# Which of two large buffers holds the block sums and which the residual rows in the last matrix product of a decoder layer

## The chip, the core and the metric

The kernel runs on one core of one Trainium2 chip. The metric is the device time of the whole kernel in microseconds (us), the median of several runs of the same program. Before the change the three runs gave 1966.43, 1971.43 and 1974.03 us, so the median is 1971.43 us.

A core has engines that run at the same time, each through its own list of instructions in order: TensorE (PE, matmul, with its weight loads shown as PEld), VectorE (DVE), ScalarE (ACT), GpSimd (POOL) and SyncE (SP). In this kernel SP, POOL and ACT also issue transfers (DMA). Engines wait for each other through semaphores.

## What is computed

The reference is one layer of a decoder on 1024 rows of 1024 float32 numbers. Everything but its last step is left as it is by the change. The last step is the end of a gated feed-forward block and a layer norm over the residual sum:

```python
def conv_ffn(h, w_up, dw_w, dw_b, w_down):
    u = causal_dwconv(h @ w_up, dw_w, dw_b)
    gate, val = jnp.split(u, 2, axis=-1)
    return (jax.nn.silu(gate) * val) @ w_down
...
ffn = conv_ffn(h, w_ffn_up[l], ffn_dw_w[l], ffn_dw_b[l], w_ffn_down[l])
h = layer_norm(DN_ALPHA * h + ffn, ln2_g[l], ln2_b[l])
```

`silu(gate) * val` is 1024 rows by 2816 channels, and `w_down` is 2816 by 1024. `h` on the right-hand side is what this page calls the residual rows.

## The kernel before

**The stages.** The kernel normalises the input, runs the mixing part in two halves of 512 rows, projects it back, then does the feed-forward block: the *up phase* (`up_first`, `up_rest`, 22 turns, one for each 128 gate channels with their value channels) and the *down phase* (`down`). Every float32 operand is split into a high part (a cast on ACT) and a low part (a subtraction on DVE), and each product is three matmuls: high times high, high times low, low times high (`mm3`, L170, L171, L172).

**The down phase.** The product with `w_down` is made with seven block products in place of eight. Rows are cut into an early and a late half, channels and output columns into two halves each. Blocks of the activations were written to memory by the up phase (`b11_scr`, `b2_scr`, `t1_scr`, `t32_scr`). The seven products (numbered 0 to 6 here) run one after the other; each has `NK` = 11 steps `k` of 128 channels, and a step is 12 matmuls of 512 columns: four row blocks `t`, three matmuls each. They accumulate in two sets of four banks: `X` (tiles named `acc`) and `Y` (tiles named `sm`, which the up phase uses too).

**One step.** `load(p, k)` (L1024) makes the operands of a step and is traced at a high priority:

- SP loads the activation block and a block of `w_down` into a raw tile `dr` of 512 KB (L1040, L1043). There are five raw tiles: three of the pool `wst` and two of the pool `up`, all shared with the up phase.
- In the products 0, 1, 4 and 5, POOL loads a second block of 256 KB into a tile called `other`, named `do` in the profile (L1049). There are four such tiles: two of the pool `up`, shared with the up phase, and two of the pool `down`.
- In product 0, DVE adds the two weight blocks into `c3[k]`; in product 1 into `c4[k]` (L1012). The sums are weights of later products: `c3` of the products 2 and 3, `c4` (after `c3` has been added) of product 6.
- ACT casts the raw tile into the high half of a weight tile `w_dn` (L1077), and DVE subtracts to get the low half (L1078). There are six weight tiles: three of the pool `wsp`, shared with the up phase, and three of the pool `down`. The steps 0, 1, 2 and every second step after that take one of `wsp`.

A raw tile can be loaded anew only when the cast, the subtraction and the addition that read it are done.

**The large buffers.** The pool `big` has two buffers of 4 MB (32 KB on each of 128 partitions). In the up phase one holds `h1b1`, which only `up_first` reads, and the other `h1b2`, which the fourth product of every turn of `up_rest` reads. `up_first` runs ahead and ends first, so the buffer of `h1b1` is given up first and the buffer of `h1b2` almost at the end of the up phase. In `down` the first large tile that is asked for takes the former, the second one the latter. Before the change these are `rows`, the 1024 residual rows (eight loads of 512 KB by POOL, L1007), and `c3`, the eleven sums of 256 KB. A third large tile, `last`, is asked for in product 6 (L1065); it holds the weights of its last four steps and takes the buffer of `c3` when all that is in it has been read.

**The pool `down`.** It lies on memory that the pool `ffq` of the up phase gives up: the block sums `h1s1` to `h1s3`, read until late in the up phase, and four small tiles `first`, done with when the last `up_first` has been stored. Its tiles are laid out in the order in which they are first asked for: ten sums of `c4`, the statistics, the gain and bias rows (`ln_g`, `ln_b`), `other`, then the weight tiles.

**The residual sum.** After product 0, `one(t)` (L1100, four DVE instructions, L1095) multiplies the early half of rows 0 to 511 by alpha and adds the bank `X[t]`. Functions of the same kind follow the other products; the last of them end in the layer norm and the stores (`ln_out`).

**What sets the order.** All loops are unrolled. A planner simulates the program at build time and puts each engine's instructions into one fixed list, higher priority first among those that could run by its simulation. On the chip each engine then goes through its list in order, so an instruction that waits holds up everything behind it on its engine. A DMA that waits for a buffer holds up the queue that issues it.

Of the kernel before, what the change touches and what calls it, by code (L numbers as in the profile page):

```python
# [8 lines left out]
F32 = mybir.dt.float32  # L9
F32R = mybir.dt.float32r  # L10
# [6 lines left out]
P = 128  # L17
D = 1024
T = 1024
HALF = 512  # L20
# [25 lines left out]
RW_ING, RW_INB, RW_1G, RW_1B, RW_2G, RW_2B = (i * D for i in range(6))  # L46
# [9 lines left out]
def kernel(  # L56
# [16 lines left out]
    V, A, G, TE, SY = nc.vector, nc.scalar, nc.gpsimd, nc.tensor, nc.sync  # L73
# [25 lines left out]
    later = statep.tile([P, P], F32, name="later")  # L99
# [42 lines left out]
    def weights(src, name, keep=None, kept=None):  # L142
        with tc.high_priority(offset=4000):
            st = wst.tile([P, D], F32, tag="st", name=f"st_{name}")
            SY.dma_start(st, src)
            w = wsp.tile([P, 2, D], F32R, tag="w", name=f"w_{name}")
            A.copy(w[:, 0, :], st)  # L147
            if kept is not None:
                SY.dma_start(w[:, 1, :].bitcast(F32), kept)
            else:  # L150
                V.tensor_tensor(  # L151
                    out=w[:, 1, :], in0=st, in1=w[:, 0, :].bitcast(F32), op=ALU.subtract
                )
            if keep is not None:
                SY.dma_start(keep, w[:, 1, :].bitcast(F32))
        return w

    def col_weights(hh, ct):
        scr = low_scr.get(ct)
        return weights(  # L160
            wcol[ct], f"c{hh}_{ct}", None if hh else scr, scr if hh else None
        )

    def big_tile(name):
        return big.tile([P, 2, KD, HALF], F32R, tag="big", name=name)
# [39 lines left out]
    def row(pl, start, n, name, tag=None, eng=SY):  # L205
        r = pl.tile([P, n], F32, tag=tag or name, name=name)
        eng.dma_start(r, prow[start : start + n].partition_broadcast(P))
        return r
# [781 lines left out]
    def down(upp, dp):  # L990
# [6 lines left out]
        def flat_big(name):  # L997
            return big_tile(name).bitcast(F32).rearrange("p i k t -> p (i k t)")

        rows, kept = flat_big("rows"), flat_big("c3")  # L1000
        c3 = [kept[:, k * HALF : (k + 1) * HALF] for k in range(NK)]
        c4 = [dp.tile([P, HALF], F32, name=f"c4_{k}") for k in range(NK - 1)]
        c4.append(upp.tile([P, HALF], F32, tag="s3", name="c4_last"))
        rs = [rows[:, t * D : (t + 1) * D] for t in range(8)]
        sts = [dp.tile([P, 2, 6], F32, name=f"st_f{t}") for t in range(8)]
        for t in range(8):
            G.dma_start(rs[t], h1_scr[t * P : (t + 1) * P, :])  # L1007
        g, b = (row(dp, w, D, n, eng=G) for w, n in ((RW_2G, "ln2_g"), (RW_2B, "ln2_b")))
        E, L = slice(0, HALF), slice(HALF, D)

        def add(dst, x, y):
            V.tensor_tensor(out=dst, in0=x, in1=y, op=ALU.add)  # L1012

        n_steps, n_raw, n_other = 0, 0, 0

        def raw(name):
            nonlocal n_raw
# [1 line left out]
            pl, tag, bufs = ((wst, "st", 3), (upp, "raw", 2))[n_raw % 5 in (1, 3)]  # L1019
            return pl.tile([P, D], F32, tag=tag, bufs=bufs, name=f"{name}_{n_raw}")  # L1020

        last = []

        def load(p, k):  # L1024

            nonlocal n_steps, n_other
            a11, a21, a12, a22 = (wdown[h * NK + k, :, cs] for h in range(2) for cs in (E, L))
            x = (
                b11_scr[k],
                b2_scr[k][:, E],  # L1030
                t32_scr[k][:, L],
                t32_scr[k][:, E],
                t1_scr[k],
                b2_scr[k][:, E],
                b2_scr[k][:, L],
            )[p]
            with tc.high_priority(offset=4000):
                st = raw("dr")
                w_st = st[:, E]
                SY.dma_start(st[:, L], x)  # L1040
                w_of = (a11, a12, a22, None, a21, a22, None)[p]
                if w_of is not None:
                    SY.dma_start(w_st, w_of)  # L1043
                o_of = (a21, a22, None, None, a22, t32_scr[k][:, L], None)[p]
                if o_of is not None:
                    n_other += 1
                    pl, tag = ((dp, "other"), (upp, "s"))[n_other % 2]
                    other = pl.tile([P, HALF], F32, tag=tag, bufs=2, name=f"do{p}_{k}")
                    G.dma_start(other, o_of)  # L1049
                if p < 2:  # L1050
                    add((c3, c4)[p][k], w_st, other)
                elif p == 2:
                    add(w_st, w_st, c3[k])
                elif p == 3:
                    w_st = c3[k]
                    add(c4[k], c4[k], c3[k])
                elif p == 4:
                    add(w_st, w_st, other)
                elif p == 5:
                    add(st[:, L], st[:, L], other)  # L1060
                else:
                    w_st = c4[k]
                if p == 6 and k >= NK - 4:
                    if not last:
                        last.append(big_tile("last").rearrange("p i k t -> p (i k t)"))  # L1065
                    w = last[0][:, (k - NK + 4) * 2 * D : (k - NK + 5) * 2 * D]
                    w = w.rearrange("p (i n) -> p i n", i=2)
                else:
                    own = n_steps % 2 and n_steps > 2
                    w = (dp if own else wsp).tile(  # L1070
                        [P, 2, D], F32R, tag="w", bufs=3, name=f"w_dn{p}_{k}"
                    )
                cuts = ((slice(0, D), st),) if w_st is not c3[k] and w_st is not c4[k] else (
                    (E, w_st), (L, st[:, L])
                )
                for cs, src in cuts:
                    A.copy(w[:, 0, cs], src)  # L1077
                    V.tensor_tensor(  # L1078
                        out=w[:, 1, cs], in0=src, in1=w[:, 0, cs].bitcast(F32), op=ALU.subtract
                    )  # L1080
            n_steps += 1
            return w
# [17 lines left out]
        def one(t):  # L1100
            own(X[t], rs[t], E, ALU.add)
# [34 lines left out]
        for p, (banks, first, then) in enumerate(products):  # L1136
            end = NK - LAST if p == 6 else NK
            for k in range(end):
                w = load(p, k)
                for t in range(4):  # L1140
                    block(banks[t], w, t, first, k)
            ws = {k: load(p, k) for k in range(end, NK)}
            for t in range(4):
                for k in ws:
                    block(banks[t], ws[k], t, first, k)
                then(t)

    def ln_out(dp, t, r, g, b, st):

# [11 lines left out]
    with pool("rows0") as pl:  # L1161
        rs = [pl.tile([P, D], F32, name=f"r0_{t}") for t in range(4)]
# [4 lines left out]
    mixT, _ = combine(1, hT, yT, accs)  # L1167
# [15 lines left out]
    upp = ctx.enter_context(pool("up"))  # L1183
# [5 lines left out]
    dp = ctx.enter_context(pool("down", side="right"))  # L1189
# [100 lines left out]
```

## Time and profile before

| what | value |
|---|---|
| runs | 1966.43, 1971.43, 1974.03 us; median 1971.43 us |
| the profiled execution's own time | 1972.21 us |
| its span (first to last instruction) | 1970.1 us |
| granted TensorE clock, mean | 0.996 |
| end of the up phase's last matmul, from the span's start | about 1751 us |
| last matmul of the kernel | about 1959 us |

The profile is of one execution. Its span lies 2.1 us under that execution's own time. It gives, for each engine, how long it was busy, a view in 40 slices, the chain of work that ended last, and groups of instructions by source line. Further views list single instructions in order of time (a timeline; the note in square brackets is how long the engine stood idle before the instruction, and what released it), sum up waits between engines, or give the busy time of each engine in stretches that the reader names. In names such as `c<-dr,do` the tile that is written stands before the arrow. A matmul is shown as 0.39 us long, but they are pipelined: in undisturbed stretches one starts every 0.227 us.

### The profile page before, as it was taken

To read this page: it belongs to the slowest core of one execution; us is meant where nothing else is said; L and a number is where in the kernel's file an instruction comes from. 1 tells how busy PE (TensorE), PEld (TensorE's weight loads), DVE (VectorE), ACT (ScalarE), POOL (GpSimd) and SP (SyncE) were. 2 spreads that over 40 slices of the span, in tenths; PEclk is the share of its full clock that TensorE was granted. 3 is DMA by queue.
4 is the path that set the end of the run, shared out by engine and by line. 5 is a ranking of instruction groups with operands and counts; after the bars stand their busy time and mean duration, and the time that the engine had idled before them with its cause. 6 is when DMAs were issued, how large, how long until landed. Compare 5 with 4: busy or idle time off the path is not lost.

```text
span 1970.1 us, 25840 instructions
## 1 busy us (share of the span) xinstructions
PE 1932.9 (98%) x9453; PEld 1575.2 (80%) x9453; DVE 1600.7 (81%) x2224; ACT 1083.8 (55%) x1617; POOL 203.1 (10%) x246
## 2 busy tenths in 40 slices
PE   9999999999899999999999999999999999999997
PEld 8888777777688788888778888888888888878886
DVE  7599999999786547898999655587788888879778
ACT  4676767653263265868775435365555555544432
POOL 0001010110310000110101040001000000121010
PEclk9999999999999999999999999999999999999999
DMA  7645455546455665555554644576455555588673
GB/s 270 221 171 198 161 206 177 166 162 202 157 187 176 215 221 182 190 184 198 178 178 148 213 162 129 169 255 227 160 166 183 175 185 184 179 293 297 201 230 125
DMA packets 128416, 378.36 MB, mean 192 GB/s; under 512 B 15104, under 2 KB 15648, under 8 KB 128288
## 3 DMA queue, kind: packets, MB, share of 16 engines
q1 hardware_dynamic: 109152, 321.63, 48.7%
q0 software_dynamic: 12800, 43.54, 6.4%
q10 hardware_dynamic: 6336, 11.54, 1.6%
q8 instruction: 74, 1.21, 0.3%
q14 instruction: 54, 0.44, 0.1%
HBM read 289.99 MB, written 86.65 MB: 191 GB/s over the span
## 4 chain that ended last, share of the span: by engine, by line
PE 71%; DVE 16%; issue 5%; DMA 5%; ACT 2%; POOL 1%; SPq 0%; DVEq 0%; ACTq 0%; POOLq 0%
PE acc L172 16%; PE acc L171 16%; PE acc L170 16%; PE sm L171 6%; PE sm L172 6%; PE sm L170 6%; DVE c L453 5%; DVE w_c L151 1%; DVE x L408 1%; DMA rstd<-nrm_scr 1%; PE sm L536 1%; DMA dr<-wdown 1%; PE sm L539 1%; DVE x L588 1%; DMA b_scr<-fo 1%
## 5 line engine op out<-in xcount | busy, mean ns | idle before, releaser
L170 PE MATMUL acc<-hT,w_c 128*128 128x512 f32 x1000 | 391.8, 392 | 0.5 <-ACT x L406 0.5
L171 PE MATMUL acc<-hT,w_c 128*128 128x512 f32 x1000 | 390.7, 391 | 0.0
L172 PE MATMUL acc<-hT,w_c 128*128 128x512 f32 x1000 | 390.1, 391 | 0.6 <-DVE w_c L151 0.5
L453 DVE SCALAR_TENSOR_TENSOR c<-v,pc,c 128x512 f32<-128x512 f32 x480 | 370.6, 798 | 7.3 <-ACT c L442 4.7
L170 PEld LDWEIGHTS acc<-hT,w_c 128*128 128x128 f32 x1000 | 187.8, 188 | 41.7 <-issue 1.9
L172 PEld LDWEIGHTS acc<-hT,w_c 128*128 128x128 f32 x1000 | 187.8, 188 | 41.2 <-DVE w_c L151 1.4
L171 PEld LDWEIGHTS acc<-hT,w_c 128*128 128x128 f32 x1000 | 187.8, 188 | 39.2 <-issue 1.1
L147 ACT CAST w_c<-st_c 128x1024 fp32r<-128x1024 f32 x128 | 133.8, 1045 | 108.5 <-PE acc L172 90.0
L515 POOL TENSOR_TENSOR ce<-ce,xbc 128x1024 f32<-128x1024 f32 x28 | 74.1, 2648 | 694.3 <-ACT ce L514 694.3
L1077 ACT CAST w_dn<-dr 128x1024 fp32r<-128x1024 f32 (+1 forms) x73 | 68.8, 944 | 87.5 <-DMA dr<-wdown 25.3
L504 ACT ACTIVATE m<-ab,acs 128x128 f32<-128x128 f32 x256 | 78.4, 390 | 48.2 <-PE sm L536 47.0
L170 PE MATMUL sm<-h1s,w_s 128*128 128x512 f32 x264 | 102.7, 389 | 0.0
L171 PE MATMUL sm<-h1s,w_s 128*128 128x512 f32 x264 | 102.7, 389 | 0.0
L172 PE MATMUL sm<-h1s,w_s 128*128 128x512 f32 x264 | 102.2, 389 | 0.0
L151 DVE TENSOR_TENSOR w_c<-st_c,w_c 128x1024 fp32r<-128x1024 f32 x64 | 79.1, 1239 | 22.3 <-ACT w_c L147 22.1
L1078 DVE TENSOR_TENSOR w_dn<-dr,w_dn 128x1024 fp32r<-128x1024 f32 (+1 forms) x73 | 78.7, 1089 | 5.3 <-ACT w_dn L1077 5.3
L408 DVE SCALAR_TENSOR_TENSOR x<-u,pc,x 128x512 f32<-128x512 f32 x96 | 76.7, 810 | 5.7 <-ACT x L406 5.7
L172 PE MATMUL acc<-h1b,w_ue 128*128 128x512 f32 x176 | 68.9, 395 | 1.5 <-DVE w_ue L151 1.5
L170 PE MATMUL acc<-h1b,w_ue 128*128 128x512 f32 x176 | 68.8, 391 | 0.0
L171 PE MATMUL acc<-h1b,w_ue 128*128 128x512 f32 x176 | 68.6, 390 | 0.0
L170 PE MATMUL sm<-h1b,w_s 128*128 128x512 f32 x176 | 68.5, 389 | 0.0
L171 PE MATMUL sm<-h1b,w_s 128*128 128x512 f32 x176 | 68.5, 389 | 0.0
(324 smaller groups left out, 4542.3 us busy)
## 6 DMA issues: line engine op xcount, KB each, us to landing
st_c<-wcol SPq DMA_DIRECT2D x128, 512.0 KB, 4.4
low_scr<-w_c SPq DMA_DIRECT2D x64, 512.0 KB, 2.9
w_c<-low_scr SPq DMA_DIRECT2D x64, 512.0 KB, 4.4
ab<-acs_scr SPq DMA_DIRECT2D x32, 512.0 KB, 4.1
dr<-wdown SPq DMA_DIRECT2D x55, 256.0 KB, 4.8
st_wo<-wo SPq DMA_DIRECT2D x24, 512.0 KB, 4.0
st_ue<-wup SPq DMA_DIRECT2D x22, 512.0 KB, 4.2
first_scr<-first ACTq DMA_DIRECT2D x44, 256.0 KB, 2.9
```

Source lines behind the costliest of these rows:

```text
L147: A.copy(w[:, 0, :], st)
L151: V.tensor_tensor(out=w[:, 1, :], in0=st, in1=w[:, 0, :].bitcast(F32), op=ALU.subtract)
L170: TE.matmul(ps, wa(0), xa(0), start=start, stop=False, skip_group_check=more)
L171: TE.matmul(ps, wa(0), xa(1), start=False, stop=False, skip_group_check=more)
L172: TE.matmul(ps, wa(1), xa(0), start=False, stop=stop, skip_group_check=more)
L408: V.scalar_tensor_tensor(out=o, in0=u[:, k : k + HALF], scalar=pc[:, wc + k : wc + k + 1], in1=o, op0=ALU.mult, op1=ALU.add,)
L453: V.scalar_tensor_tensor(out=accs[i], in0=v[:, k : k + HALF], scalar=pc[:, wc + k : wc + k + 1], in1=accs[i], op0=ALU.mult, op1=ALU.add,)
L504: A.activation(out=m[:, h, :], in_=ab[:, h, :], func=AF.Relu, scale=-1.0, bias=acs[:, c, 8 * g + h : 8 * g + h + 1],)
L515: G.tensor_tensor(out=ce, in0=ce, in1=CT[:, cs].unsqueeze(1).to_broadcast([P, 8, P]), op=ALU.mult)
L536: TE.matmul(o, xs[:, h * HP : (h + 1) * HP], m[:, h, :], start=True, stop=first)
L1077: A.copy(w[:, 0, cs], src)
L1078: V.tensor_tensor(out=w[:, 1, cs], in0=src, in1=w[:, 0, cs].bitcast(F32), op=ALU.subtract)
```

## The change

`c3` now takes the large buffer that is given up first and `rows` the other one. `c3` needs 22 of its 32 KB, so the first two sums of `c4` move into the same buffer, behind the eleven of `c3`. The four `other` tiles are now all of the pool `down`; the two of the pool `up` are no longer used for this. To place them, the first weight tile of `down` (`first_own`) is asked for ahead of them, which puts the `other` tiles at the end of the pool, on the memory of the four `first` tiles. The weight tiles then lie on the memory of `h1s2` and `h1s3`.

The residual rows and the gain and bias rows are no longer loaded at the beginning of `down` but in product 1, after `load(1, 2)`; a dependence without a semaphore (`issue_after`) keeps their ten DMAs behind the `other` load of that step in POOL's list. `one(t)` moves from the end of product 0 to step 7 of product 1.

```diff
+    def issue_after(later, earlier):
+
+        tc.add_manual_dep(
+            later.ins,
+            earlier.ins.name,
+            mybir.DependencyInfo(mybir.DependencyClass.NoSync, mybir.DependencyReason.DATA),
+            reason="issue order",
+        )
...
-        rows, kept = flat_big("rows"), flat_big("c3")
+        kept, rows = flat_big("c3"), flat_big("rows")
         c3 = [kept[:, k * HALF : (k + 1) * HALF] for k in range(NK)]
-        c4 = [dp.tile([P, HALF], F32, name=f"c4_{k}") for k in range(NK - 1)]
+        c4 = [kept[:, k * HALF : (k + 1) * HALF] for k in range(NK, NK + 2)]
+        c4 += [dp.tile([P, HALF], F32, name=f"c4_{k}") for k in range(2, NK - 1)]
...
-        for t in range(8):
-            G.dma_start(rs[t], h1_scr[t * P : (t + 1) * P, :])
-        g, b = (row(dp, w, D, n, eng=G) for w, n in ((RW_2G, "ln2_g"), (RW_2B, "ln2_b")))
+        g, b = (dp.tile([P, D], F32, name=n) for n in ("ln2_g", "ln2_b"))
+        first_own = dp.tile([P, 2, D], F32R, tag="w", bufs=3, name="w_dn_own")
+
+        def load_rows():
+            for t in range(8):
+                i = G.dma_start(rs[t], h1_scr[t * P : (t + 1) * P, :])
+                issue_after(i, others[-1])
+            for r, start in ((g, RW_2G), (b, RW_2B)):
+                i = G.dma_start(r, prow[start : start + D].partition_broadcast(P))
+                issue_after(i, others[-1])
...
-                    n_other += 1
-                    pl, tag = ((dp, "other"), (upp, "s"))[n_other % 2]
-                    other = pl.tile([P, HALF], F32, tag=tag, bufs=2, name=f"do{p}_{k}")
-                    G.dma_start(other, o_of)
+                    other = dp.tile([P, HALF], F32, tag="other", bufs=4, name=f"do{p}_{k}")
+                    others.append(G.dma_start(other, o_of))
...
                     w = (dp if own else wsp).tile(
                         [P, 2, D], F32R, tag="w", bufs=3, name=f"w_dn{p}_{k}"
-                    )
+                    ) if n_steps != 3 else first_own
...
             for k in range(end):
                 w = load(p, k)
+                if p == 1 and k == 2:
+                    load_rows()
+                if p == 1 and k == 7:
+                    for t in range(4):
+                        one(t)
                 for t in range(4):
                     block(banks[t], w, t, first, k)
...
-                then(t)
+                if p:
+                    then(t)
```

More of the change, by code (lines that the diff above doesn't have):

```diff
@@ L1012, in add @@
             V.tensor_tensor(out=dst, in0=x, in1=y, op=ALU.add)
-        n_steps, n_raw, n_other = 0, 0, 0
+        n_steps, n_raw = 0, 0
         def raw(name):
@@ L1020, in raw @@
             return pl.tile([P, D], F32, tag=tag, bufs=bufs, name=f"{name}_{n_raw}")
-        last = []
+        last, others = [], []
         def load(p, k):
-            nonlocal n_steps, n_other
+            nonlocal n_steps
             a11, a21, a12, a22 = (wdown[h * NK + k, :, cs] for h in range(2) for cs in (E, L))
```

## The prediction

> **What bounds the kernel now.** I read the page first.
>
> ```profile
> PE 1932.9 (98%) x9453; PEld 1575.2 (80%) x9453; DVE 1600.7 (81%) x2224; ACT 1083.8 (55%) x1617; POOL 203.1 (10%) x246
> PE 71%; DVE 16%; issue 5%; DMA 5%; ACT 2%; POOL 1%; SPq 0%; DVEq 0%; ACTq 0%; POOLq 0%
> ```
>
> PE is busy for 98% of the span, and the change takes no matmul away. It can win only where PE stands still or runs slowly in the down phase, and in the tail behind the last matmul. The table of windows shows where that is. Its columns are the length, the busy time (count) of PE, PEld, DVE, ACT and POOL, the granted clock, the busy share of the DMA engines and GB/s.
>
> ```profile
> 1736.00:1747.40 11.40, 9.06 (x32) 6.68 (x31) 8.09 (x8) 6.23 (x7) 1.95 (x5) 0.85 0.33 128
> 1747.40:1753.00 5.60, 5.60 (x26) 4.61 (x26) 4.78 (x6) 3.32 (x4) 1.36 (x3) 1.00 0.92 264
> 1753.00:1780.00 27.00, 24.97 (x106) 19.09 (x105) 23.59 (x28) 10.62 (x10) 8.28 (x16) 1.00 0.96 333
> 1780.00:1810.00 30.00, 29.63 (x132) 24.20 (x130) 29.38 (x39) 12.19 (x12) 5.48 (x10) 1.00 0.98 334
> 1810.00:1840.00 30.00, 30.00 (x133) 24.64 (x132) 27.14 (x38) 14.37 (x19) 0.00 (x0) 1.00 0.60 185
> ```
>
> The last row is undisturbed: 133 matmuls in 30 us, one in 0.226 us, so a step of twelve takes 2.7 us. At that rate the first row would hold 50.5 matmuls and holds 32 (18.5 missing, 4.2 us), the third 119.7 and holds 106 (13.7 missing, 3.1 us), the fourth lacks one (0.2 us). That is 7.5 us in all, 0.38% of the kernel: the ceiling of what steadier feeding can win.
>
> The first stop, from the timelines of POOL, ACT, DVE and PE, with the step of the critical chain in the third row:
>
> ```profile
> 1717.32 4.28 POOL L1007 DMA_DIRECT2D rows<-h_scr  x8 [10.28 <-PE acc L172]
> 1723.77 0.54 POOL L982 DMA_DIRECT2D b_scr<-fo  x1 [1.44 <-DVE fo L970]
> 1723.77 12.28 DMA b_scr<-fo
> 1736.21 1.15 ACT L955 ACTIVATE fo<-fug,pc 128x1024 f32<-128x1024 f32 x1 [1.78 <-DMA b_scr<-fo]
> 1738.82 1.04 ACT L1077 CAST w_dn<-dr 128x1024 fp32r<-128x1024 f32 x1 [0.41 <-PE acc L172]
> 1739.85 1.28 DVE L959 SCALAR_TENSOR_TENSOR fo<-fug,pc,fo 128x1024 f32<-128x1024 f32 x1
> 1741.05 1.22 DVE L1078 TENSOR_TENSOR w_dn<-dr,w_dn 128x1024 fp32r<-128x1024 f32 x1
> 1738.39 0.39 PE L172 MATMUL acc<-w_dn 128*128 128x512 f32 x1
> 1739.91 1.20 PE L170 MATMUL acc<-w_dn 128*128 128x512 f32 x4 [1.14 <-ACT w_dn L1077]
> 1742.32 0.69 PE L171 MATMUL acc<-w_dn 128*128 128x512 f32 x1 [1.21 <-DVE w_dn L1078]
> 1743.23 0.63 PE L171 MATMUL acc<-w_dn 128*128 128x512 f32 x1
> 1743.66 0.63 PE L172 MATMUL acc<-w_dn 128*128 128x512 f32 x1
> 1742.00:1746.00 4.00, 3.68 (x9) 2.90 (x10) 3.25 (x4) 0.79 (x2) 0.45 (x1) 0.57 0.01 2
> ```
>
> POOL issues eight row loads at 1717; the store of `b_scr` behind them on its queue takes 12.28 us; ACT's L955 waits for the tile; DVE's L959 and, behind them in its list, the second step's subtraction come late. PE waits twice, and then the granted clock is 0.57 and matmuls start every 0.43 us.
>
> The second stop comes from the sums, by the waits of SP's queue, its timeline, DVE's and PE's:
>
> ```profile
> SPq L1040 <- DVE c L1012: 47.1, 12, 17.8
> 1733.00 0.32 SPq L1040 DMA_DIRECT2D dr<-b_scr  x1
> 1752.28 0.32 SPq L1040 DMA_DIRECT2D dr<-b_scr  x1
> 1751.52 1.29 DVE L1012 TENSOR_TENSOR c<-dr,do 128x512 f32<-128x512 f32 x2 [0.41 <-PE sm L172]
> 1768.96 0.50 PE L171 MATMUL acc<-w_dn 128*128 128x512 f32 x1 [1.61 <-DVE w_dn L1078]
> 1725.00:1730.00 5.00, 5.00 (x23) 4.13 (x22) 1.22 (x2) 1.18 (x2) 1.08 (x2) 1.00 1.04 417
> 1740.00:1745.00 5.00, 3.79 (x11) 2.69 (x12) 5.00 (x5) 1.62 (x2) 0.10 (x1) 0.75 0.01 2
> ```
>
> The first sum starts only when the up phase's last matmul has released `c3`'s buffer. Until then all five raw tiles are held, SP loads nothing from 1733 to 1752, and the DMA engines, at 417 GB/s when rows and raw tiles came together, move 2 GB/s at 1740. Afterwards loads run at 333 GB/s and PE starves.
>
> **The change part by part.** The sum is made against the profiled execution's own 1972.21 us, 0.8 us above the median of the runs.
>
> *The sums' buffer.* The row loads waited for an `acc` matmul (first row of the first stop) and started at 1717.32, so that buffer is free there. The additions, 21 and one of about 0.69 us, are the same; the first five can run from about 1725, where DVE is busy 1.22 of 5 us. Their `other` tiles now lie on tiles that the up phase has done with. The second raw load after 1733 then waits for casts rather than for sums: about 10 us sooner, four steps. PE's stop at 1768 was of late data, so I take all 3.1 us as won. Ends: 0 (the cast holds the raw tile as long) and 3.1. SP issues as many loads as before.
>
> *The first stop.* Without rows ahead of it the store's landing no longer holds L955; a 256 KB store of the same kind usually lands in 2.3 us (third row of the next fence). But the cast of step 1 waited for PE (0.41, `acc`): steps 0 to 2 follow each other through the `wsp` tiles that the up phase leaves free. So 1739.91 − 1738.39 − 0.23 = 1.3 us stay. The subtraction can start with the cast's end at 1739.86 in place of 1741.05: the second wait shrinks from 1.4 to about 0.3. I count on the clock staying full, since after the single wait of 1.61 us at 1768.96 it did (1.00 in the row of 1753). What is won is 4.2 − 1.3 − 0.3 = 2.6 us, with ends of 0 and 4.2.
>
> The Trainium skill (TensorE: Matmul & The Clock Gate, "Part 1: The HAM clock gate") has the clock halved after an idle window of about 3.4 us. Here it fell after two waits of 1.3 and 1.4 us with matmuls between them, so the trace is stricter than the page. By the page alone the remaining stop keeps its clock too; if the drop came all the same, the term would be 1.0 and not 2.6.
>
> *Rows in product 1.* These rows price it:
>
> ```profile
> L1007 POOL DMA_DIRECT2D rows<-h_scr x8 | 4.3, 543 | 10.3 <-PE acc L172 10.3
> ln_g<-prow POOLq DMA_DIRECT2D x1, 512.0 KB, 6.0
> DMA to landing us min/median/max: 2.3/2.3/2.8
> 1734.63 0.56 POOL L1049 DMA_DIRECT2D do<-wdown  x1 [6.87 <-ACT w_dn L1077]
> 1773.04 1.16 POOL L1049 DMA_DIRECT2D do<-wdown  x2 [1.84 <-DVE c L1012]
> ```
>
> Ten DMAs of 512 KB, 5.24 MB, now pass POOL's queue behind the `other` of step (1, 2), which was issued at about 1773.6 and should be at about 1763. Issue costs POOL 10 × 0.54 = 5.4 us, which PE does not see; the transfer takes 5.24 MB / 417 GB/s = 12.6 to 5.24 / 333 = 15.7 us. The `other` tiles of steps (1, 3) onward queue behind it. A transfer behind eight row loads took 12.28 us; four `other` tiles are a lead of 4 × 2.7 = 10.9 us. So the addition of step (1, 3) is up to 12.28 − 10.9 = 1.4 us late by that row, 15.7 − 10.9 = 4.8 us by the slow rate, and not at all if the planner mixes the loads. DVE's list stands still behind a late addition, the subtractions that PE needs among them. I take 1.4 lost, the row of the same kind; ends 0 and 4.8.
>
> An `other` load that waits for its tile holds POOL, as at 1734.63, and the up phase's last memset and stores stand behind it. With all four tiles free early that wait goes, and I put it at 0.
>
> `one(t)`, four instructions of 0.68 us, moves seven steps or about 20 us later; rows issued at 1763 have landed by then, and bank `X` is not written again before product 2. Cost 0; if rows were late, product 2 would wait as long.
>
> *The tail.* `last` takes the buffer of `c3`, in which two sums are now read until product 6:
>
> ```profile
> 1855.45 0.62 ACT L1077 CAST last<-c 128x512 fp32r<-128x512 f32 x1 [0.65 <-DVE w_dn L1078]
> 1921.40 0.69 DVE L1078 TENSOR_TENSOR w_dn<-c,w_dn 128x512 fp32r<-128x512 f32 x1
> 1925.04 0.69 DVE L1078 TENSOR_TENSOR w_dn<-c,w_dn 128x512 fp32r<-128x512 f32 x1 [1.15 <-ACT w_dn L1077]
> 1927.50 0.69 DVE L1078 TENSOR_TENSOR last<-dr,last 128x512 fp32r<-128x512 f32 x1 [1.17 <-ACT last L1077]
> 1928.00:1936.00 8.00, 8.00 (x37) 6.60 (x37) 8.00 (x16) 5.95 (x10) 0.00 (x0) 1.00 0.27 81
> 1954.30 0.69 DVE L1095 SCALAR_TENSOR_TENSOR rows<-rows,acc 128x512 f32<-128x512 f32 x1 [0.78 <-PE acc L172]
> ```
>
> Four casts and four subtractions that ran at 1855 must wait for the subtraction of the second sum, 1921.40: 4 × 0.6 = 2.4 us of DVE work in front of a stretch where DVE is full (8.00 of 8). Its holes of 1.15 and 1.17 us take nearly all of that, and 0.78 is idle at 1954. Cost 0 to 2.4; I take 0.3.
>
> Sum: −2.6 − 3.1 + 1.4 + 0.3 = −4.0; 1972.21 − 4.0 = **1968.2 us**.
>
> **The rivals.** A measurement of this kernel can tell about 0.5%, 9.9 us, from no change.
>
> *All stops go and rows cost nothing*: the planner, no longer held by the sums, puts up-phase matmuls between steps 0 and 1. −7.5: 1964.7 us. For it: POOL and DMA idle at 1740. Against it: the cast's wait for PE.
>
> *It does not do what it says*: weight tiles take the place of the sums in holding the raw tiles, and only the store's delay goes: −2.6 + 1.7 for rows and tail, 1971.3 us. For it: one `wsp` tile serves three steps.
>
> *Slower, by DMA rate.* From 1736 to 1810 the windows moved 11.4×128 + 5.6×264 + 27×333 + 30×334 = 21.9 MB. Rows add 4.2 MB (gain and bias were in it already), the early `other` tiles take about 1 MB out: 25.1 MB. In 74.0 us that needs 339 GB/s, and 377 to end 7.5 us sooner. The stretch ran at 334 with the engines 0.98 busy; if that is its limit, loads need 75.2 us, +1.2, and with DVE waiting for (1, 3) 4.8 and the tail 2.4: +8.4, 1980.6 us. It decides below 339 GB/s. Against it: 417 at 1725 with both queues full.
>
> The Trainium skill (DMA: Bandwidth & Descriptors, "Bandwidth") names about 358 GB/s as one core's share of memory; 417 here is above it, and the measurement decides. By 358 the 25.1 MB would take 70.1 us, −3.9, which is near the forecast.
>
> **How the numbers follow.** Forecast (−6 to −2) 0.5; all stops go 0.15; no effect (−2 to +3) 0.22; slower by DMA 0.13. The range reaches from the second case, less 3 us for the spread of the runs (1966.43 to 1974.03), to the middle of the last: 1961.7 to 1976. Only the tails of the second and fourth cases pass 9.9 us: faster 0.06, same 0.88, slower 0.06.
>
> **What would show it.** Right: `c<-dr,do` before 1730; `dr` loads between 1736 and 1750 and GB/s above 200 there; L955 not waiting for `b_scr`; no PE wait over 0.5 us at 1768. Wrong: DVE or PE waiting for `do` behind rows in product 1; a granted clock under 1.00 after 1736; `last<-c` on DVE pushing the layer norms past PE's end.

## The result and the profile after

Nine runs of the kernel after had a median of 1977.08 us, nine of the kernel before beside them 1969.95 us: 1.0034 times as long, with a 95% interval of 1.0024 to 1.0044, or, by that ratio, 6.7 us (4.7 to 8.7) more. A second measurement gave 1.0022 [1.0012, 1.0032], 4.3 us. The change costs about a quarter of a per cent; 1968.2 us and the whole range (up to 1976.0) were below it.

The windows of the kernel after, at the times of those shown of the kernel before (its last row, 1810 to 1840, is still disturbed here):

```profile
1736.00:1747.40 11.40, 11.08 (x49) 9.19 (x50) 10.01 (x11) 7.02 (x8) 3.46 (x7) 1.00 0.53 162
1747.40:1753.00 5.60, 5.60 (x27) 4.62 (x25) 5.60 (x7) 2.21 (x3) 1.91 (x4) 1.00 0.97 323
1753.00:1780.00 27.00, 26.38 (x116) 21.38 (x115) 23.20 (x29) 10.42 (x10) 9.79 (x19) 1.00 1.00 370
1780.00:1810.00 30.00, 23.51 (x89) 17.19 (x88) 21.52 (x29) 8.31 (x8) 6.56 (x12) 0.89 0.97 358
1810.00:1840.00 30.00, 28.94 (x126) 23.05 (x125) 27.02 (x36) 14.11 (x19) 0.00 (x0) 1.00 0.61 199
...
1725.00:1730.00 5.00, 5.00 (x24) 4.14 (x23) 1.23 (x1) 2.88 (x4) 0.00 (x0) 1.00 0.13 53
1740.00:1745.00 5.00, 5.00 (x24) 4.14 (x23) 3.61 (x5) 4.02 (x5) 2.12 (x5) 1.00 0.81 261
1800.00:1805.00 5.00, 4.96 (x13) 3.90 (x14) 4.55 (x6) 2.09 (x2) 0.61 (x2) 0.55 1.04 396
```

The first and third rows hold 49 and 116 matmuls where the kernel before had 32 and 106: both of its stops are nearly gone. The fourth holds 89 where the kernel before had 132: 43 matmuls or 9.7 us are missing there. The gain came, and more than the gain was lost 40 us later.

To set kernels side by side without the scatter of the first 1690 us, I take one matmul before the down phase, the same by count in each (it starts at 1689.7 us in the kernel before, at 1686.7 in the kernel after), and count from there: by how much the starts of the next 330 matmuls are further apart than 0.2267 us each (*both old stops*, up to some 30 matmuls before the end of product 0), the same for the 270 after them (*products 1 and 2*, from there to some 24 matmuls before the end of product 2), and from the start of the last matmul to the span's end (*tail*). All in us, each from one profiled execution, which need not be a typical one of its kernel:

| kernel | both old stops | products 1 and 2 | tail | fixed matmul to end | ratio to before, 95% interval |
|---|---|---|---|---|---|
| before | 7.8 | 0.9 | 10.8 | 280.5 | 1 |
| after | 0.9 | 13.2 | 11.4 | 286.4 | 1.0034 [1.0024, 1.0044] |
| after, again (after2) | 1.0 | 12.5 | 12.0 | 286.4 | 1.0022 [1.0012, 1.0032] |
| rows_now | 8.0 | 1.7 | 11.4 | 282.1 | 1.0006 [0.9995, 1.0016] |
| old_others | 0.8 | 11.6 | 12.4 | 285.7 | 1.0007 [0.9996, 1.0018] |
| old_others2 | 0.8 | 11.4 | 11.5 | 284.6 | 1.0007 [0.9996, 1.0017] |
| act_rows | 1.0 | 13.3 | 12.4 | 287.6 | 1.0038 [1.0025, 1.0051] |
| spread1 | 0.8 | 10.3 | 11.5 | 283.5 | 1.0024 [1.0013, 1.0034] |
| half_dose | 0.8 | 8.7 | 11.4 | 281.8 | 1.0009 [0.9996, 1.0022] |
| half_spread | 1.0 | 7.9 | 13.0 | 286.3 | 1.0006 [0.9995, 1.0017] |
| fifth_spread | 0.9 | 3.7 | 12.3 | 277.7 | 0.9994 [0.9981, 1.0007] |
| staged | 1.0 | 7.8 | 12.8 | 282.5 | 1.0004 [0.9995, 1.0012] |
| paced | 0.9 | 6.4 | 13.2 | 282.3 | 0.9995 [0.9982, 1.0008] |
| best | 0.8 | 3.3 | 11.0 | 276.0 | 0.9951 [0.9936, 0.9966] |
| best_nodo | 0.8 | 0.3 | 10.8 | 273.7 | 0.9953 [0.9940, 0.9967] |
| best2 | 0.8 | 0.0 | 11.0 | 274.9 | 0.9958 [0.9944, 0.9972] |

So the kernel after wins 6.9 us at the old stops, loses 12.2 in the products 1 and 2 and 0.6 in the tail: +5.9, twice, beside +6.7 and +4.3 by the runs. (Beyond the columns, half_spread has 3.4 us, best2 2.2, paced 1.0 and best_nodo 0.9 of stops after product 2, which I did not follow.)

In three kernels a stop between the end of the first column and the end of product 0 stands in the second: 0.9 us in the kernel after, 2.2 in half_spread and 0.7 in fifth_spread. In each of them PE waits there for the cast of a raw tile that had landed before the first row load was issued. In half_spread, by the timelines of ACT, POOL and PE:

```profile
1762.56 1.05 ACT L1090 CAST w_dn<-dr 128x1024 fp32r<-128x1024 f32 x1 [1.23 <-DMA dr<-wdown]
1762.68 0.54 POOL L1155 DMA_DIRECT2D rows<-h_scr  x1
1763.66 1.21 PE L179 MATMUL sm<-w_dn 128*128 128x512 f32 x4 [1.83 <-ACT w_dn L1090]
```

These stops are therefore not the rows' doing. Without them the second column is 12.2, 5.8 and 3.0 us for these three.

**What is left of the old stops.** The timelines of POOL, DVE and PE in the kernel after:

```profile
1734.81 0.10 POOL L941 MEMSET fuv<- 128x2 f32 x1 [11.21 <-DVE fo L968]
1739.21 0.54 POOL L989 DMA_DIRECT2D b_scr<-fo  x1 [4.30 <-DVE fo L979]
1739.74 2.17 POOL L1065 DMA_DIRECT2D do<-wdown  x4
1736.32 0.50 PE L179 MATMUL sm<-h1s,w_s 128*128 128x512 f32 x1 [0.53 <-ACT fuv L953]
1743.81 0.69 DVE L1030 TENSOR_TENSOR c<-dr,do 128x512 f32<-128x512 f32 x1 [0.99 <-DMA do<-wdown]
```

Until 1765 PE waits once, 0.53 us, for an up-phase instruction on ACT. But the sums did not become early: all four `other` loads stand in POOL's list behind a memset and a store of the up phase, which wait for DVE until 1739.21, so the first sum runs at 1743.81 and not before 1730. The hole in the transfers moved forward (53 GB/s from 1725 to 1730) and did not close; at 1740 the rate is 261 and no longer 2 GB/s.

**The new stop.** The timelines of POOL, SP, ACT, DVE and PE in the kernel after:

```profile
1764.74 3.33 POOL L1021 DMA_DIRECT2D rows<-h_scr  x6
...
1776.87 0.55 POOL L1065 DMA_DIRECT2D do<-wdown  x1 [1.68 <-DMA rows<-h_scr]
1774.63 0.43 SPq L1061 DMA_DIRECT2D dr<-wdown  x1
1793.38 0.32 SPq L1058 DMA_DIRECT2D dr<-b_scr  x1
1774.63 1.05 ACT L1093 CAST w_dn<-dr 128x1024 fp32r<-128x1024 f32 x1 [2.89 <-DMA dr<-wdown]
1778.59 1.05 ACT L1093 CAST w_dn<-dr 128x1024 fp32r<-128x1024 f32 x1 [2.90 <-DMA dr<-wdown]
...
1790.41 1.05 ACT L1093 CAST w_dn<-dr 128x1024 fp32r<-128x1024 f32 x1 [2.92 <-DMA dr<-wdown]
1798.94 1.04 ACT L1093 CAST w_dn<-dr 128x1024 fp32r<-128x1024 f32 x1 [7.49 <-DMA dr<-wdown]
1792.63 0.68 DVE L1030 TENSOR_TENSOR c<-dr,do 128x512 f32<-128x512 f32 x1
1800.04 2.07 PE L179 MATMUL sm<-w_dn 128*128 128x512 f32 x4 [5.17 <-ACT w_dn L1093]
```

While rows move, casts come 3.9 us apart ((1790.41 − 1774.63) / 4), each ended by the landing of its raw tile; a step needs one every 2.7 us. The `other` load of step (1, 3) is issued behind the ten loads, at 1776.87, and lands 13.9 us later; its sum, behind a subtraction in DVE's list, runs only at 1792.63. (POOL issues even the ten loads slowly. In all these traces neither POOL nor SP ever has more than eight transfers under way; from 1768.83 to 1786.71 there are eight, and each issue of POOL waits for a landing. Whether the chip or the program sets this is not shown.) Until the sum has run the raw tiles are held and SP issues nothing from 1774.63 to 1793.38. The next cast starts at 1798.94, PE stands for 5.17 us, and then its clock is 0.55 for 5 us. The view of the transfers from 1768 to 1791 (packets, MB and busy share, for POOL's queue q0 and SP's queue q1):

```profile
DMA packets 3330, 9.29 MB, mean 404 GB/s; under 512 B 392, under 2 KB 392, under 8 KB 3330
...
q0 software_dynamic: 1813, 6.53, 71.7%
q1 hardware_dynamic: 1517, 2.75, 31.8%
```

The engines are full, at 404 GB/s. SP gets 2.75 MB in 23 us, 120 GB/s, where 512 KB in 2.72 us are 193.

### The profile page after: what moved, and what is told of

Same layout as the page of the kernel before. It is cut to its first block, busy times and chain, and to the rows that moved or that the text cites. A ratio compares the mean times of both kernels' runs of the same rounds, so it can differ in the third digit from the quotient of the medians.

```text
span 1973.1 us, 25851 instructions
## 1 busy us (share of the span) xinstructions
PE 1933.8 (98%) x9453; PEld 1575.1 (80%) x9453; DVE 1598.3 (81%) x2224; ACT 1083.0 (55%) x1617; POOL 207.1 (10%) x246
## 4 chain that ended last, share of the span: by engine, by line
PE 64%; DVE 20%; DMA 7%; issue 5%; ACT 3%; POOL 1%; SPq 0%; DVEq 0%; POOLq 0%; ACTq 0%
PE acc L181 15%; PE acc L179 15%; PE acc L180 15%; DVE c L462 6%; PE sm L181 5%; PE sm L179 5%; PE sm L180 5%; DMA dr<-wdown 3%; DVE w_dn L1094 2%; DVE w_c L151 1%; DVE x L417 1%; PE sm L545 1%; DMA dr<-b_scr 1%; DMA rstd<-nrm_scr 1%; PE sm L548 1%
```

## The experiments

**Theory T1:** the loss is the 5.24 MB that POOL's queue now carries in product 1. It can act by the bytes alone, by the share that SP's queue gets beside POOL's, or because the `other` loads stand behind the burst. **Rival R2:** the moved `other` tiles are at fault. First I undid one part at a time.

**rows_now** loads rows, gain and bias at the beginning of `down`, as before the change:

```diff
-        def load_rows():
+        for t in range(8):
+            G.dma_start(rs[t], h1_scr[t * P : (t + 1) * P, :])
...
-                if p == 1 and k == 2:
-                    load_rows()
```

> Change: only the swap of the buffers and of the tiles is kept; rows, gain and bias are loaded at the beginning of the down phase as in the kernel before (now into the buffer given up last), and `one` follows product 0 again. T1: the loss moves with the loads: POOL's list now waits for the late buffer to about 1747, so the row loads and every `other` load behind them start there; the stop at 1800 goes, but a stop of 3 us or more appears between 1747 and 1780; in all at least as slow as the kernel after (ratio 1.002 to 1.006). R2: the same loss as the kernel after, still at 1800. Should the late place in product 1 have been the whole fault, ratio below 0.999.

Measured: 1.0006 [0.9995, 1.0016]. The timelines of POOL, DVE and PE in this kernel show why my picture of it was wrong:

```profile
1712.43 4.26 POOL L1020 DMA_DIRECT2D rows<-h_scr  x8 [10.28 <-PE acc L181]
1745.40 0.69 DVE L1027 TENSOR_TENSOR c<-dr,do 128x512 f32<-128x512 f32 x1 [0.60 <-DMA do<-wdown]
1756.17 1.51 PE L179 MATMUL acc<-w_dn 128*128 128x512 f32 x4 [2.84 <-ACT w_dn L1090]
```

The rows wait 10.28 us for an `acc` matmul, as in the kernel before, and start early: they have the buffer given up first, which leaves `c3` the other one. By this trace a large tile takes its buffer when it is first used, not when it is asked for; loading the rows first undid the swap too. So this is the kernel before with the moved `other` and `c4` tiles only: both old stops are back (8.0 us), 1.7 us are lost in the products 1 and 2 against 0.9 before, and the runs show neither a gain nor a cost of those tiles by themselves. That they serve only beside the swap stays possible.

**old_others** keeps the rest and undoes the `other` tiles:

```diff
-                    other = dp.tile([P, HALF], F32, tag="other", bufs=4, name=f"do{p}_{k}")
+                    pl, tag = ((dp, "other"), (upp, "s"))[(len(others) + 1) % 2]
+                    other = pl.tile([P, HALF], F32, tag=tag, bufs=2, name=f"do{p}_{k}")
```

> Change: the `other` tiles lie as in the kernel before, two of the pool of the up phase and two of the pool `down`; the rest of the change is kept. T1: the loss between 1784 and 1805 stays (a PE stop of 4 us or more near 1800, behind a late cast), ratio 1.002 to 1.005. R2: the stop is gone and the ratio falls to 0.998 or less.

Measured: 1.0007 [0.9996, 1.0018], below what T1 gave, but in the trace the loss is all there: 11.6 us in the products 1 and 2, with this stop in PE's timeline:

```profile
1800.26 2.07 PE L179 MATMUL sm<-w_dn 128*128 128x512 f32 x4 [6.92 <-ACT w_dn L1094]
```

Trace and ratio did not agree, so this kernel and the kernel after were both run once more (old_others2, after2):

> The kernel with the `other` tiles in their old places once more, since its one profile (13 us of PE stops after 1690) and its ratio (1.0007) did not agree. If the profile was typical: ratio 1.002 or more here. If the ratio was: a profile with under 10 us of PE stops after 1690, and the move of the `other` tiles has a part in the loss of the kernel after.

> The kernel after itself once more, with a second profile. T1 (the 5.24 MB on POOL's queue cost product 1 its data): again a PE stop of 3 us or more near 1800 and casts about 3.9 us apart before it; from a fixed matmul at 1700 to the end 4 to 8 us more than in the kernel before; ratio 1.002 to 1.005. If that stop was an accident of one execution: none above 1 us, and the ratio still 1.002 or more for another reason.

Measured: 1.0007 [0.9996, 1.0017] again with 11.4 us lost in the trace, and 1.0022 with 12.5. Neither branch came whole: the ratio stayed low, and so much was lost in the trace all the same. The stop near 1800 is in four profiles of four, so it is no accident of one execution, and it needs no moved tiles: R2 falls as its cause. From the fixed matmul to the end the two traces of `old_others` are 0.7 and 1.8 us shorter than those of the kernel after; the runs say 2.8 us in the medians of the same chip. The profiled executions of `old_others` were long ones of their kernel, 1975.86 us (the longest of twelve; median 1970.62) and 1975.62 (the fourth longest of twelve; median 1972.35), while that of the kernel after was the shortest of its nine (1974.79). So the traces may show more loss than most executions of `old_others` have, and some of the ratio of the kernel after may lie in those tiles; how much stays open.

**act_rows** takes the ten loads off POOL's queue:

```diff
-                i = G.dma_start(rs[t], h1_scr[t * P : (t + 1) * P, :])
-                issue_after(i, others[-1])
+                issue_after(A.dma_start(rs[t], h1_scr[t * P : (t + 1) * P, :]), casts[-1])
```

> Change: the ten loads of rows, gain and bias are issued on ACT's queue, behind the cast of step (1, 2), so that no `other` load stands behind them on POOL's. If what costs is that the `other` loads stand behind the rows (hold): the `other` of (1, 3) lands within 4 us of its issue, SP does not stop for 19 us, the PE stop at 1800 is under 2 us, ratio 0.998 to 1.000. If what costs is the share of the DMA engines that 4 KB packets take from SP's 2 KB ones (share): SP still gets about 137 GB/s against the 193 it needs while rows are moving, casts still come every 4 us there, and a PE stop of 3 us or more stays, ratio 1.002 or more. ACT's casts may come later by ten issues of about 0.1 to 0.5 us each under both.

Measured: 1.0038 [1.0025, 1.0051], 13.3 us lost. No `other` load stands behind the rows on their queue, and the loss is as large. The view of the transfers of this kernel, 1768 to 1791 (q10 is ACT's queue):

```profile
q10 hardware_dynamic: 1150, 4.23, 46.2%
q1 hardware_dynamic: 1370, 2.48, 29.7%
q0 software_dynamic: 736, 2.44, 27.1%
```

SP gets 2.48 MB in 23 us, 108 GB/s, less than in the kernel after. The standing behind on POOL's queue is not needed for the loss. ACT's own list was held in places, so its 13.3 us are not of one cause.

**staged** leaves 1 MB in product 1, the early halves of rows 0 to 511 that `one` reads, and issues 4.2 MB in product 2:

```diff
-                if p == 1 and k == 2:
-                    load_rows()
+                if (p, k) in ((1, 2), (2, 2)):
+                    load_rows(p - 1)
```

> Change: after `load(1, 2)` only the early halves of rows 0 to 511 are loaded (1 MB, all that `one` reads); the other 4.2 MB (late halves, rows 512 to 1023, gain and bias) follow `load(2, 2)`, where POOL's queue has no `other` loads. Theory T1 (5.24 MB on POOL's queue inside product 1 take DMA share from SP and hold the `other` of step (1, 3) behind them): the PE stop of 5.3 us at 1800 and the half clock after it go, no PE wait above 1 us between 1780 and 1805, 4 to 6 us below the kernel before (ratio 0.997 to 0.998). Rival R2 (the moved `other` tiles are the cause): the stop stays, ratio about 1.003.

Measured: 1.0004 [0.9995, 1.0012]; the stop of 5 us at 1800 is gone, as T1 had it, but its ratio did not come: 7.8 us are lost, nearly all after 1800. PE's timeline, and the view of the transfers from 1797 to 1813, when the second part moves:

```profile
1804.33 0.77 PE L180 MATMUL acc<-w_dn 128*128 128x512 f32 x1 [2.46 <-DVE w_dn L1099]
1813.16 0.50 PE L180 MATMUL acc<-w_dn 128*128 128x512 f32 x1 [1.48 <-DVE w_dn L1099]
```

```profile
DMA packets 2388, 6.41 MB, mean 401 GB/s; under 512 B 292, under 2 KB 292, under 8 KB 2388
...
q0 software_dynamic: 1196, 4.23, 66.8%
q1 hardware_dynamic: 1192, 2.18, 36.6%
```

Here both queues are full all the time, and they move the same number of packets, 1196 and 1192; POOL's are twice as large, so it gets 4.23 MB and SP 2.18 (136 GB/s). The Trainium skill (DMA: Bandwidth & Descriptors, "Queues, rings and completion order") says that a DMA engine takes turns between the queues that have work, packet by packet; this trace agrees. PE stops there although product 2 needs no `other` loads, only SP's 193 GB/s. Whether the share is the reason, the next run asks.

**paced** puts those 4.2 MB on SP's queue, one load after every first or second step:

```diff
+        paced = {(2, k): (rs[k][:, HALF:], h1_scr[k * P : (k + 1) * P, HALF:]) for k in range(4)}
+        for i, at in enumerate(((2, 4), (2, 6), (2, 8), (2, 10))):
+            paced[at] = (rs[4 + i], h1_scr[(4 + i) * P : (5 + i) * P, :])
...
+                if (p, k) in paced:
+                    with tc.high_priority(offset=4000):
+                        issue_after(SY.dma_start(*paced[p, k]), raws[-1])
```

> Change against `staged`: the late 4.2 MB are no longer issued in one go on POOL's queue, but one load behind the raw tile of every first or second step of the products 2 and 3 on SP's queue; the early halves of rows 0 to 511 stay on POOL behind step (1, 2). If the share by packets is what costs (one 4 KB packet of POOL for one 2 KB packet of SP while both queues are full): the PE stops of `staged` between 1800 and 1820 (7 us in all) go, ratio 0.996 to 0.998. If the bytes themselves are too many for the DMA engines there: a loss of 4 us or more stays in the products 2 and 3, ratio about 1.000.

Measured: 0.9995 [0.9982, 1.0008] and 6.4 us lost, 1.4 less than `staged`. The share by packets is at most a small part of what `staged` lost; the stops stay. My reading, which no run tests by itself, is that the raw tiles come out of product 1 without a lead, and row loads between them keep it so.

**spread1, half_dose, half_spread, fifth_spread** then separate the bytes from the burst. In spread1 all 5.24 MB stay in product 1, with an `other` load between any two row loads. half_dose leaves rows 0 to 511 (2.1 MB) there as a burst, half_spread the same 2.1 MB spread, fifth_spread only their early halves (1.05 MB) spread; the rest goes to SP's queue later (where it falls into product 3 the planner put two loads side by side).

```diff
+        spread = {(1, 2 + t): [(rs[t], h1_scr[t * P : (t + 1) * P, :])] for t in range(8)}
...
+                for dst, of in spread.get((p, k), ()):
+                    with tc.high_priority(offset=4000):
+                        issue_after(G.dma_start(dst, of), others[-1])
```

> Change: the ten loads stay on POOL's queue in product 1, but one row load stands behind the `other` load of each of the steps 2 to 9, and gain and bias behind that of step 10; nothing else differs from the kernel after. Hold (the `other` of (1, 3) behind all ten loads stops SP): without the burst no PE stop above 2 us in product 1 and at most 2 us lost against the kernel before, ratio 0.998 to 1.001. Bytes (5.24 MB at about 0.4 MB per us in a stretch where the DMA engines have nothing to spare, wherever they stand in the queue): the loss is spread over more and smaller stops but stays 8 us or more between 1765 and 1825, ratio 1.002 to 1.004.

> Change: after step (1, 2) POOL loads only the whole rows 0 to 511 (2.1 MB); rows 512 to 1023, gain and bias follow in product 3 on SP's queue, one load behind the raw tile of every second step. Bytes: a loss between 1765 and 1825 in proportion, 2.1 of 5.24 MB times the 13 us of the kernel after, about 5 us; ratio 0.999 to 1.001. Hold or burst with a threshold: under 2 us lost, since four loads pass within the lead of the `other` tiles; ratio 0.997 to 0.998.

> Change against `half_dose`: the whole rows 0 to 511 (2.1 MB) stay in product 1 on POOL's queue, but one load behind the `other` load of each of the steps 2 to 5 instead of four behind that of step 2. Hold: the four loads in a row were what kept the `other` of (1, 3) away, so most of the 8.6 us that `half_dose` lost between its second stop and product 2 goes, under 3 us stay, ratio 0.997 to 0.999. Bytes: 2.1 MB at 0.4 MB per us are 5.2 us wherever they stand, 5 us or more stay, ratio 0.9995 to 1.0015.

> Change: only the early halves of rows 0 to 511 (1.05 MB) are loaded in product 1, one behind the `other` load of each of the steps 2 to 5; everything else follows on SP's queue from step 4 of product 2 on, as in `best2`. Bytes in proportion: 2.6 us lost between 1765 and 1825 (in `best2` nothing), ratio 0.996 to 0.998. A lead of the raw tiles that takes up a small dose: under 1 us lost, ratio as `best2` plus the 0.6 us of the tail, 0.9955 to 0.997.

Measured: 1.0024 [1.0013, 1.0034], 1.0009 [0.9996, 1.0022], 1.0006 [0.9995, 1.0017] and 0.9994 [0.9981, 1.0007], with 10.3, 8.7, 7.9 and 3.7 us lost in the products 1 and 2. The windows of spread1:

```profile
1753.00:1780.00 27.00, 27.00 (x120) 22.08 (x119) 25.15 (x31) 10.51 (x10) 10.34 (x19) 1.00 1.00 370
1780.00:1810.00 30.00, 24.87 (x99) 17.46 (x98) 24.83 (x33) 7.36 (x8) 7.06 (x13) 1.00 1.03 389
```

Without a burst the transfers run at 389 GB/s with the engines full, and PE still misses 33 matmuls from 1780 to 1810. The losses without the last matmuls of product 0 are 10.1, 8.7, 5.8 and 3.0 us. So the burst is worth 12.2 or 12.5 − 10.1, 2 to 2.5 us at 5.24 MB, and 8.7 − 5.8 = 2.9 us at 2.1 MB. The rest grows with the bytes: 3.0 us for 1.05 MB, 5.8 for 2.1, 10.1 for 5.24, that is 2.8, 2.7 and 1.9 us per MB, where the transfer itself takes 2.5 us per MB at 404 GB/s. In the traces the two smaller doses are thus near the proportion (2.6 and 5.2 us), and "nothing for a small dose" did not come; the ratio of fifth_spread was above both branches. spread1 and half_spread also hold between 1 and 2 us of half clock behind waits of 2.31 and 2.17 us. These are single executions, and in the runs the three smaller doses can't be told from the kernel before.

The bytes do not act through the transfers of the moment alone. More than half of what the three smaller doses lose falls into product 2, and there DVE is full and the DMA engines need not be. The window and the longest wait of PE in half_dose:

```profile
1800.00:1810.00 10.00, 6.93 (x28) 5.03 (x28) 9.88 (x15) 3.14 (x3) 0.55 (x1) 1.00 0.60 195
1803.19 0.50 PE L180 MATMUL acc<-w_dn 128*128 128x512 f32 x1 [1.96 <-DVE w_dn L1096]
```

Product 2 begins at 1800 in half_dose and in best_nodo (below), but the last addition into `c4` runs at 1803.06 here and at 1797.45 there. Raw tiles that come late in product 1 leave DVE with additions to make up for in product 2. These kernels also differ from `best_nodo` in where `one` stands on DVE and where `c4` and the `other` tiles lie; how much of the loss is which, no run tells apart.

**best, best_nodo, best2** load no rows in the full stretch. The early halves of rows 0 to 511 lie in the free 8 KB behind `c3` and are loaded when that buffer comes free; `one` follows product 0 again and writes its result to the rows' place. All ten `c4` tiles of the pool are back in it, so that only `c3` and these halves hold the buffer of `last`. The rest goes over SP's queue as in `paced`. `best` also puts the `other` loads of steps 0 to 2 on SP's queue, ahead of step 4's raw tile, and their sums ahead of the next subtractions; `best_nodo` leaves that out; `best2` starts the paced loads at step 4 of product 2.

```diff
+        rE = [kept[:, k * HALF : (k + 1) * HALF] for k in range(NK, NK + 4)]
+        c4 = [dp.tile([P, HALF], F32, name=f"c4_{k}") for k in range(NK - 1)]
...
+        for t in range(4):
+            G.dma_start(rE[t], h1_scr[t * P : (t + 1) * P, :HALF])
...
-            own(X[t], rs[t], E, ALU.add)
+            V.scalar_tensor_tensor(
+                out=rs[t][:, E], in0=rE[t], scalar=ALPHA, in1=X[t], op0=ALU.mult, op1=ALU.add
+            )
...
+                    others.append((SY if p == 0 and k < 3 else G).dma_start(other, o_of))
```

> Change: as `paced`, but the early halves of rows 0 to 511 lie behind the sums in the buffer given up first and are loaded early (`one` writes its result into the rows' own place and follows product 0), all ten `c4` tiles are back in the pool `down` (so nothing but `c3` holds the buffer of `last`), the `other` tiles are in their old pools, and the loads for the sums of steps 0 to 2 go to SP's queue ahead of the raw tile of step 4, with their sums ahead of the next subtractions. T1: no PE stop above 1 us after 1736, tail as in the kernel before, 5 to 8 us below it, ratio 0.996 to 0.9975. If the order of the first steps does not help: ratio 0.998 to 1.000 with PE stops between 1740 and 1790.

> Change: `best` without the early loads and sums of the steps 0 to 2 (all `other` loads on POOL in the planner's order again). If the early sums give a part of what `best` won: 1.5 us or more slower than `best`, ratio 0.996 to 0.998. If they give nothing and rows and tail are all: the ratio of `best`, 0.994 to 0.996.

> Change: `best` with the paced loads later: late halves of rows 0 to 511 behind the steps 4 to 7 of product 2, rows 512 to 1023, gain and bias in product 3. Bytes: the 2.4 us of PE stops that `best` still has between 1805 and 1815 go, since no row load then falls into the time in which the raw tiles catch up; 1 to 3 us below `best`, ratio 0.993 to 0.995. If those stops come from the additions of product 2 on DVE and not from the loads: the same as `best`.

Measured: 0.9951 [0.9936, 0.9966], 0.9953 [0.9940, 0.9967] and 0.9958 [0.9944, 0.9972]: all three beat both kernels and are 8 to 10 us below the kernel before; `best` is under its range and best2 over. POOL's timeline and the windows of best_nodo:

```profile
1715.52 2.17 POOL L1020 DMA_DIRECT2D c<-h_scr  x4 [10.28 <-PE acc L181]
```

```profile
1753.00:1780.00 27.00, 27.00 (x121) 22.36 (x120) 26.79 (x34) 11.73 (x12) 7.11 (x13) 1.00 1.00 350
1780.00:1810.00 30.00, 30.00 (x134) 24.82 (x134) 28.08 (x39) 10.11 (x10) 3.83 (x7) 1.00 0.97 343
1810.00:1840.00 30.00, 29.98 (x133) 24.49 (x132) 25.17 (x35) 15.86 (x24) 0.28 (x1) 1.00 0.70 230
```

PE has its 121, 134 and 133 matmuls, with the engines as full as in the kernel before: product 1 leaves little room beside its own data. The early sums give nothing (`best` is no better than `best_nodo`), and the later pace of `best2` none that the runs show, though its trace is the only one with nothing lost there. The tail is back at 10.8 to 11.0. In the traces these kernels are 4.5 to 6.8 us below the kernel before, in the runs 8.3 to 9.7; that difference is open.

## Why the prediction was wrong

*The first stop and the sums' buffer.* Predicted −2.6 and −3.1, together −5.7; measured 7.8 to 0.9, −6.9, and 0.8 to 1.0 us stay in every kernel with the swap. L964, the old L955, no longer waits for a store; where 1.6 us should stay, one stop of 0.69 us did (the wait of 0.53 and a slow start), and for another cause. The 3.1 came in full in the second profile and but for the 0.9 us at 1765 in the first, though not by early sums: `c<-dr,do` ran at 1743.81, 7.7 us sooner than before, and it was enough that it no longer waited for the up phase's last matmul. That the `other` loads would free POOL's list was wrong: the memset and the store of the up phase stood ahead of them.

*Rows in product 1: the step that failed.* I had taken 1.4 us with an end of 4.8; it was 11.4 in the first profile (12.2 less 0.8 as before) and 11.5 in the second. The step set one delayed transfer (12.28 us) against a lead of four `other` tiles (10.9 us), as if the one load behind the rows were all that could come late. That load itself landed 26 us after the first row load was issued (1764.74 to 1790.79), and PE's own raw tiles came late as well, which the sum had left out. What the runs show in its place: with the rows out of product 1, 0.3 us are lost in the products 1 and 2 (best_nodo; 0.0 in best2 and 3.3 in best). With rows in it, SP gets 120 GB/s of the 193 it needs and casts come 3.9 us apart; loads that are spread cost 1.9 to 2.8 us a MB (spread1, half_spread, fifth_spread), in part through additions that DVE must make up for in product 2; loads in a burst, with the `other` loads held behind them, cost 2 to 3 us more; and the half clock after a 5 us stop is in it. How the cost per MB divides between transfers and DVE stays open.

*The rival that was near.* "Slower, by DMA rate" put the kernel at 1980.6 us and the point that decides at 339 GB/s. From 1736 to 1810 the kernel after moved 11.4 × 162 + 5.6 × 323 + 27 × 370 + 30 × 358 = 24.4 MB in 74 us, 330 GB/s: below that point. I gave it 0.13 because of 417 GB/s at 1725. That row shows how fast the engines run with both queues full, not whose bytes they carry: at 404 GB/s SP got 120. But the rival was near in part by luck. It took 334 GB/s for the engines' limit, and they ran at 404; the mean is low because they moved 162 up to 1747, and 264 from 1791 to 1800, after SP had issued nothing for 19 us. And 2.4 of its 8.4 us were for a tail that cost 0.6 and 1.2.

*The tail.* Predicted 0.3 (0 to 2.4), measured 0.6 and 1.2. DVE's timeline of the kernel after shows the late casts' subtractions:

```profile
1924.34 1.90 DVE L1094 TENSOR_TENSOR last<-c,last 128x512 fp32r<-128x512 f32 x3
...
1931.50 0.69 DVE L1094 TENSOR_TENSOR last<-dr,last 128x512 fp32r<-128x512 f32 x1 [2.26 <-ACT last L1093]
```

The place is the one foreseen. With nothing of `c4` in that buffer the tail is as before (`best_nodo`), though the other kernels with it reach 13.2, so that not all of it is these casts.

Of the marks set down, L964 and loads of `dr` between 1736 and 1750 were right, and the missing wait at 1768 in one profile (the other has 0.62 us at 1765); the rate from 1736 to 1750 was 187 GB/s and not above 200, and `c<-dr,do` before 1730 was wrong; and two of the marks against came, a PE wait behind rows in product 1 and a clock under 1.00. And the runs told more than the 0.5% that I had counted on: the interval reaches 0.1% to either side.

## What to carry to other kernels

Price a moved transfer by the stretch that it moves into, queue by queue: where the engines were full, each MB cost 1.9 to 2.8 us here, about its transfer time, whatever lead one tile had. A buffer that comes free early is worth most to loads that can fill a hole in the transfers; put there what fits, and feed the rest through the queue that the critical loads use, after the full stretch, as the three best kernels here do. When a swap of buffers forces a load to move, measure the swap and the move apart.

## What the hardware showed that I had not expected

Two full queues share the engines by packets and not by bytes: 1196 to 1192 packets, but 4.23 to 2.18 MB, in 16 us. And a transfer lands later the more is queued with it: a `dr` load of 256 KB that was issued before the rows took 8.60 us in the kernel after, one issued behind them 15.68, as the critical chain has it:

```profile
1762.00 8.60 DMA dr<-wdown
...
1774.63 15.68 DMA dr<-wdown
```

The clock also halved after shorter waits than the 5.17 us here. Matmuls started 0.43 us apart behind single waits of PE of 2.46 us (staged), 2.31 (spread1) and 2.17 (half_spread), but not behind one of 1.96 us (half_dose). These are four single cases and no threshold.
